# Up-projections of a two-layer diffusion backbone: the order in which ScalarE, VectorE and GpSimd prepare operands and weights

## The chip, the cores and the metric

The kernel runs on one core of one Trainium2 chip. The metric is the device time of one execution in microseconds (us), the median of several runs; less is better. The engines are TensorE (PE, matmuls), VectorE (DVE), ScalarE (ACT), GpSimd (POOL) and SyncE (SP), which issues the DMAs. Each engine works through its own queue in order.

## What is computed

A backbone of two layers over 1024 latent tokens and, in layer 0, 256 context tokens, all fp32, of width 1024. Each layer has an attention mixer and then a channel mixer with a convolution over neighbouring tokens, each behind a modulated RMSNorm:

```python
def conv_ffn(h, w_up, conv_w, conv_b, w_down):
    a = h @ w_up                       # 1024 -> 2 x 2816
    g, u = a[..., :D_FF], a[..., D_FF:]
    T = g.shape[1]
    half = CONV_W // 2                 # CONV_W = 3
    gp = jnp.pad(g, ((0, 0), (half, half), (0, 0)))
    acc = conv_b + gp[:, 0:T] * conv_w[0]
    for j in range(1, CONV_W):
        acc = acc + gp[:, j:j + T] * conv_w[j]
    return (jax.nn.silu(acc) * u) @ w_down

# in each layer i, behind the attention mixer:
ml = (silu(c) @ w_mod[i] + b_mod[i]).reshape(B, N_MOD, 1, D)
xl = xl + ml[:, 5] * conv_ffn(modulate(xl, ml[:, 3], ml[:, 4]), ffn_w_up[i], ...)
if not last:                           # layer 0 alone: the context tokens too
    xc = xc + mc[5] * conv_ffn(modulate(xc, mc[3], mc[4]), ffn_w_up[i], ...)
```

The change touches the product `h @ w_up` of both layers.

## The kernel before

**Products.** A value of fp32 is held as two parts of reduced precision, high and low, and a product is three matmuls: high by high, high by low, low by high (`mm3`, L72). The high part is a cast, the low part the value less its high part. The up-projection works on 22 blocks f of 128 features of g and the same of u. For the latent tokens one block is a 2 x 2 product (g and u by two halves of 512 tokens), computed by Strassen's scheme in Winograd's form with seven products of twelve matmuls each instead of eight. The operand's four sums t1 to t4 are made once, in the head, by four objects `Parts` (one for each row of blocks j): `first` makes four sums in place on DVE (L1598 to L1601), `high` a high half on ACT (L1606, L1608), `low` a low half on DVE (L1616, L1618). The weights' sums s1 to s4 are made for each block: GpSimd adds (L1694), ACT takes the high part (L1698), DVE the low one (L1702). The table of products is

```python
PROD = {1: ("a11", "b11", "x"), 2: ("a12", "b21", "x"), 6: ("s2", "t2", "y"), 7: ("s3", "t3", "y"), 4: ("a22", "t4", "y"), 5: ("s1", "t1", "z"), 3: ("s4", "b22", "z")}
```

with the weight, the operand and the group x, y or z of PSUM banks that takes the sum. There are eight banks, used in a ring. In a trace `y<-h,s3h` is product 7, `z<-h,s4h` product 3, `x<-h,a1h` product 1 or 2, `p<-` a plain product. In layer 0 the context tokens have two plain products in each block.

**A turn.** `Up.turn(f)` writes the order of one block: products 6, 5, 7, then product 1 of the next block, 3, 2 of the next block, 4. Between them stand the steps that bring the sums out of PSUM: `c21` (L1997), `u2` (L1979), `u3` (L1988), `c22` (L1991), `c12` (L1994) on DVE, `s1` (L1975) and `c11` on ACT; the convolution `conv` (ACT, L2004) and `conv2` (DVE, L2008 and L2009), `silu` (ACT, L2012) and `mix` (silu by u; GpSimd for the latent tokens, DVE for the context's, L2015). A finished block is stored to `d_act`. The next block's weights are loaded as two halves `raw` (1024 columns each, two buffers); `ahigh` makes a1h on GpSimd and a2h on ACT, `alow` makes a1l and a2l on DVE (L1683). Product 7 needs u2 to have read its bank, product 3 needs c22 to have read its bank, product 1 of the next block needs a1h and a1l.

**mod().** Layer 0's turns also compute columns of the modulation for later: a DMA brings a block of w_mod into the one buffer `wm`, DVE reduces it (L321, one or two reductions for a block), and GpSimd finishes with steps on one column (L326). `mod()` stands three times in a turn of layer 0.

**The head.** `Up.head` does blocks 0 and 1 with plain products, while the norm in front is still being finished: `n1.quick` makes the last of the operand, and then the `Parts` are made and the turns begin with f = 2. Its `f0` and `f1` are blocks 0 and 1; `gate` (L1969) and `upper` (L1972) copy plain products out of PSUM on ACT. In front of the head stand the last steps of the attention's out-projection, the norm's totals and roots (`n1.split`, `n1.total`, `n1.root`), the splitting of the first two weights `w0[0]` and `w0[1]` (L111 is a low part) and `up.second`, which loads and splits the weights of block 1.

**Order.** Head and turns lie in a region whose order on PE, DVE, ACT and GpSimd is that of the code. The DMA queue of SP lies outside of it and is ordered by a scheduler from the program.

## Time and profile before

| | |
|---|---|
| time, median of 3 runs | 2918.14 us (2915.58 to 2920.52) |
| profiled execution | 2918.13 us, span 2916.3 us, mean granted clock 0.986 |
| TensorE busy | 2793.6 us, 96% of the span, 14654 matmuls |
| DVE, ACT, GpSimd busy | 2201.5 (75%), 1242.3 (43%), 1075.8 (37%) |
| half of a weight block, raw, from issue to landing | 3.3 us in the median of 86 |
| modulation block, wm, from issue to landing | 3.6 us in the median of 72 |

The span runs from the first to the last instruction of the profiled execution; all places named in the text are us from its start. The up-projection of layer 0 lies at about 703 to 1320, that of layer 1 at about 2192 to 2655. An engine's busy time says only that it worked; what a change can win is seen from where TensorE waited, and for whom. The granted clock is a share of TensorE's full speed: where it is under 1, matmuls take longer.

### The profile page before, as it was taken

The numbers are of one execution on the slowest core, as the hardware profiler recorded it, in microseconds if no ns is written. First come the engines' busy times: TensorE is split into PE (matmuls) and PEld (weight loads), VectorE is DVE, ScalarE is ACT, GpSimd is POOL, SyncE is SP. The second block draws the span as 40 slices with busy tenths as digits, with TensorE's granted clock in tenths as the row PEclk, the third lists the DMA queues.
The fourth block names the chain that finished last, engine by engine and source line by source line (L and its number), as shares of the span: only waits on it lengthen the run. The fifth ranks groups of instructions, "written<-read, shape, count | busy, mean of one in ns | idle before, by whom it ended". The sixth has DMA issues, their size and how long they took to land.

```text
span 2916.3 us, 40138 instructions
## 1 busy us (share of the span) xinstructions
PE 2793.6 (96%) x14654; PEld 2319.8 (80%) x14654; DVE 2201.5 (75%) x3646; ACT 1242.3 (43%) x2520; POOL 1075.8 (37%) x1066
## 2 busy tenths in 40 slices
PE   7988999999899999999999998999999999999997
PEld 3857888887778878888888776999977788887886
DVE  5688888879677777668767888888757666558766
ACT  5525888724323323331101444888734333333104
POOL 2142444762234444431101534444331444542112
PEclk9999999999999999999999999999999999999998
DMA  6144001372133433454211110000041222226311
GB/s 227 70 141 137 15 24 58 111 252 100 47 128 106 135 121 105 136 176 165 87 57 48 44 37 30 1 1 1 23 140 51 84 76 84 80 88 234 98 58 58
DMA packets 97230, 264.89 MB, mean 91 GB/s; under 512 B 11909, under 2 KB 21061, under 8 KB 96905
## 3 DMA queue, kind: packets, MB, share of 16 engines
q1 hardware_dynamic: 97032, 262.33, 26.8%
q8 instruction: 115, 1.88, 0.3%
q14 instruction: 83, 0.67, 0.1%
HBM read 212.53 MB, written 49.75 MB: 90 GB/s over the span
## 4 chain that ended last, share of the span: by engine, by line
PE 56%; DVE 11%; ACT 3%; issue 3%; DMA 2%; POOL 1%; DVEq 0%; SPq 0%; ACTq 0%; POOLq 0%
PE d L72 18%; PE y L72 7%; PE x L72 6%; PE z L72 5%; PE p L72 5%; PE pv L1277 3%; PE b L72 3%; DMA wm<-in_wmod 2%; PE T L1264 2%; PE S L1197 1%; PE qk L72 1%; PE S L1199 1%; PE S L1198 1%; DVE x L2008 1%; DVE x L321 1%
## 5 line engine op out<-in xcount | busy, mean ns | idle before, releaser
L2091 DVE SCALAR_TENSOR_TENSOR x<-d,mod,x 128x512 f32<-128x512 f32 (+1 forms) x352 | 254.7, 735 | 94.9 <-PE d L72 92.4
L1246 POOL TENSOR_SCALAR p<-p,sm 128x1280 f32<-128x1280 f32 x128 | 171.3, 1339 | 288.1 <-DVE sm L1245 201.0
L1267 DVE TENSOR_TENSOR tl<-T,th 128x512 fp32r<-128x512 f32 x328 | 225.5, 688 | 46.9 <-ACT th L1266 41.9
L1277 PE MATMUL pv<-th,v 128*128 128x256 f32 x976 | 254.1, 309 | 1.4 <-ACT vo L1406 1.0
L1220 DVE TENSOR_REDUCE mx<-S 128x1 f32<-128x512 f32 (+1 forms) x400 | 234.0, 585 | 10.9 <-PE S L1199 3.7
L72 PE MATMUL d<-act,wh 128*128 128x512 f32 (+1 forms) x832 | 232.0, 365 | 0.0
L1266 ACT CAST th<-T 128x512 fp32r<-128x512 f32 x328 | 192.2, 586 | 84.4 <-PE T L1264 77.0
L2074 ACT CAST act<-act 128x512 fp32r<-128x512 f32 (+1 forms) x110 | 61.4, 577 | 382.8 <-PE d L72 250.4
L72 PE MATMUL b<-h,wh 128*128 128x512 f32 (+1 forms) x752 | 206.6, 362 | 6.0 <-DVE h L489 4.1
L1694 POOL TENSOR_TENSOR x<-raw 128x512 f32<-128x512 f32 x80 | 119.5, 1493 | 237.2 <-DMA raw<-in_wup 136.1
L2015 POOL TENSOR_TENSOR su<-x,su 128x512 f32<-128x512 f32 x78 | 125.9, 1616 | 218.3 <-ACT x L2012 123.7
L72 PE MATMUL x<-h,a1h 128*128 128x512 f32 x624 | 201.2, 404 | 5.0 <-POOL a1h L1678 5.0
L1975 ACT COPY su<-x 128x512 f32<-128x512 f32 x40 | 23.5, 586 | 411.0 <-PE x L72 378.9
L1264 PE MATMUL T<-ident,p 128*128 128x128 f32 x1280 | 193.0, 272 | 1.6 <-POOL p L1246 1.6
L1264 PEld LDWEIGHTS T<-ident,p 128*128 128x128 f32 x1280 | 156.5, 140 | 34.9 <-POOL p L1246 3.3
L1277 PE MATMUL pv<-tl,v 128*128 128x256 f32 x656 | 177.4, 282 | 0.0
L1277 PEld LDWEIGHTS pv<-th,v 128*128 128x128 f32 x976 | 173.4, 189 | 2.4 <-ACT vo L1406 1.5
L72 PEld LDWEIGHTS d<-act,wh 128*128 128x128 f32 x832 | 149.7, 189 | 27.1
L72 PEld LDWEIGHTS b<-h,wh 128*128 128x128 f32 x752 | 132.9, 189 | 35.9 <-DVE h L489 5.5
L72 PE MATMUL d<-act,wl 128*128 128x512 f32 (+1 forms) x416 | 151.8, 365 | 0.0
L72 PEld LDWEIGHTS x<-h,a1h 128*128 128x128 f32 x624 | 120.5, 194 | 34.3 <-POOL a1h L1678 7.1
L72 PE MATMUL x<-h,a1l 128*128 128x512 f32 x312 | 128.1, 411 | 19.4 <-DVE a1l L1683 19.4
(515 smaller groups left out, 8198.0 us busy)
## 6 DMA issues: line engine op xcount, KB each, us to landing
raw<-in_wup SPq DMA_DIRECT2D x86, 512.0 KB, 3.3
wm<-in_wmod SPq DMA_DIRECT2D x72, 512.0 KB, 3.6
act<-d_act SPq DMA_DIRECT2D x88, 256.0 KB, 3.5
raw<-in_wdn SPq DMA_DIRECT2D x44, 512.0 KB, 4.1
raw<-in_wout SPq DMA_DIRECT2D x32, 512.0 KB, 3.4
d_act<-su SPq DMA_DIRECT2D x22, 640.0 KB, 3.5
d_act<-su SPq DMA_DIRECT2D x22, 512.0 KB, 2.8
raw<-in_win SPq DMA_DIRECT2D x20, 512.0 KB, 3.6
```

The costliest lines, as they stand in the source:

```text
L72: PE.matmul(out, w, x, start=first and i == 0, stop=last and i == n - 1, skip_group_check=more)
L321: V.tensor_tensor_reduce(out=out, in0=wm, in1=silc[w], op0=ALU.mult, op1=ALU.add, scale=1.0, scalar=bmod[:, l, i : i + 1], accum_out=mod[l ...
L1220: V.reduce_max(mx[:, j : j + 1], s, axis=AX.X)
L1246: P.tensor_scalar(out=self.p, in0=self.p, scalar1=sm[:, 3:4], scalar2=1.0, op0=ALU.mult, op1=ALU.mult)
L1264: PE.transpose(tb[:, (2 * j + i) * 128 : (2 * j + i) * 128 + 128], rows[i].p[:, c : c + 128], ident)
L1266: S.copy(hi, tb)
L1267: V.tensor_sub(lo, tb, f32(hi))
L1277: PE.matmul(out[0], st, mv, start=(u + j == 0 and x == 0), stop=(u + j == n - 1 and x == len(ops) - 1))
L1694: eng.tensor_tensor(out=t, in0=self.src(f, x), in1=self.src(f, y), op=op)
L2015: eng.tensor_mul(self.s_of(c), self.t[c], self.s_of(c) if u is None else u)
L2074: S.copy(hi, f32(lo))
L2091: V.scalar_tensor_tensor(out=x, in0=b, scalar=mod[self.l, c // 2][:, 40 + d : 41 + d], in1=x, op0=ALU.mult, op1=ALU.add)
```

## The change

No instruction is added or removed; four places of code are written in another order.

- In front of the head, `w0[1]`'s split moves ahead of `n1.split`, and `n1.total` and `n1.root` move ahead of `mod2(3)` and `up.second`.
- In the head, after the quick norm, only the first copies are made (three in layer 0, one in layer 1); then come all four `Parts`, with the copies of f1's gate between the second and the third; then the other copies, a1's two parts, and f1's upper copies.
- In a turn, the load of the next block's first half and its a1h on GpSimd move ahead of the two mixes, and a1l moves to right behind `u2`.
- On SP, in five turns of layer 0, the load of raw's second half now stands ahead of the store to `d_act`.

```diff
--- before.py
+++ after.py
@@ -1782,31 +1782,30 @@
                 b.append(lambda b=self.plain(w1[0], 2): f1.gate(2, b))
             n1.rest()
             n1.quick(())
-            for f in b:
-                f()
-            f0.gate(1, self.plain(w[0], 1, n1.QUICK))
-            f0.upper(1, self.plain(w[1], 1))
-            self.a_tiles()
-            self.ahigh(2, 0, S)
+            b.append(lambda b=self.plain(w[0], 1, n1.QUICK): f0.gate(1, b))
+            b.append(lambda b=self.plain(w[1], 1): f0.upper(1, b))
+            for _ in range(3 if ctx else 1):
+                b.pop(0)()
             parts = [Parts(self, j) for j in range(4)]
             big = lambda: tuple(hp.tile([128, 512], F32R, name="h", tag="h", bufs=HB) for _ in "hl")
             small = lambda: tuple(np_.tile([128, 512], F32R, name="t", tag=t, bufs=tmp.bufs[t]) for t in self.pairs.pop(0))
-            for p in parts[:2]:
+            for j, p in enumerate(parts):
                 p.first()
-                p.high(2, big())
-                p.high(1, big())
-                p.low(2)
-                p.low(1)
+                if j == 2:
+                    for _ in range(2 if ctx else 1):
+                        b.pop(0)()
+                for t in (2, 1):
+                    p.high(t, big() if j < 2 else small())
+                for t in (2, 1):
+                    p.low(t)
+            for f in b:
+                f()
+            self.a_tiles()
+            self.ahigh(2, 0, S)
+            self.alow(2, 0)
             f1.upper(0, self.plain(w1[1], 0))
             if ctx:
                 f1.upper(2, self.plain(w1[1], 2))
-            self.alow(2, 0)
-            for p in parts[2:]:
-                p.first()
-                p.high(2, small())
-                p.high(1, small())
-                p.low(2)
-                p.low(1)
             if ctx:
                 t = self.sp.tile([128, 1024], F32, name="wm", tag="wm", bufs=1)
                 f0.temps = [t[:, :512], t[:, 512:]]
@@ -1863,13 +1862,15 @@
                 down.load(0)
                 for e in (0, 1):
                     down.act_load(e)
+            if n:
+                self.load(n, 0)
+                self.ahigh(n, 0, P)
             if f > 2:
                 old.mix(1)
                 old.mix(0)
                 old.store()
             self.alow(f, 1)
             if n:
-                self.load(n, 0)
                 self.load(n, 1)
             else:
                 down.load(1)
@@ -1877,6 +1878,8 @@
             if not n:
                 down.act_split(0)
             me.u2()
+            if n:
+                self.alow(n, 0)
             if f == 2:
                 old.rest()
                 me.c11(True)
@@ -1884,9 +1887,6 @@
                 if f == 3 and not ctx:
                     self.fs[0].rest()
                 self.mod()
-            if n:
-                self.ahigh(n, 0, P)
-                self.alow(n, 0)
             self.product(f, 7)
             if not n:
                 down.act_split(1)
@@ -2246,13 +2246,13 @@
     o.update(15, 1)
     up.spill(7, 1)
     last()
+    w0[1] = w0[1]()
     n1.split()
+    up.plain(w0[0], 0, range(6, 8), b00)
+    n1.total()
+    n1.root()
     mod2(3)
     up.second(1)
-    up.plain(w0[0], 0, range(6, 8), b00)
-    n1.total()
-    w0[1] = w0[1]()
-    n1.root()
     up.second(0)
     up.head(w0, b00, n1)
     for f in range(2, NF):
@@ -2880,12 +2880,12 @@
     o.update(15, 1)
     up.spill(7, 1)
     last()
+    w0[1] = w0[1]()
     n1.split()
-    up.second(1)
     up.plain(w0[0], 0, range(6, 8), b00)
     n1.total()
-    w0[1] = w0[1]()
     n1.root()
+    up.second(1)
     up.second(0)
     up.head(w0, b00, n1)
     for f in range(2, NF):
```

ACT in the head of layer 0, behind the quick norm. `p` is a plain product in PSUM, g and su are the rows of a block, L1606 and L1608 write high halves of the `Parts`:

```order
-L1969 COPY g<-p 128x512
-L1969 COPY g<-p 128x256
-L1969 COPY g<-p 128x512
-L1972 COPY su<-p 128x512
-L1676 CAST a1h<-raw 128x1024
 L1606 ACTIVATE h<-x_6972,mod_65 128x512
 L1608 CAST h<-x_6972 128x512
 L1606 ACTIVATE h<-x_6973,mod_65 128x512
 L1608 CAST h<-x_6973 128x512
-L1972 COPY su<-p 128x512
-L1972 COPY su<-p 128x256
+L1969 COPY g<-p 128x512
```

Four copies and a1h, which stood ahead of the first high halves, now stand behind them.

ACT in the head of layer 1, at the end of the `Parts`:

```order
 L1606 ACTIVATE t<-x_12641,mod_66 128x512
 L1608 CAST t<-x_12641 128x512
+L1969 COPY g_21844<-p 128x512
+L1972 COPY su_21841<-p 128x512
+L1676 CAST a1h<-raw 128x1024
+L1972 COPY su<-p 128x512
 L1969 COPY g<-p 128x512
 L1698 CAST s2h<-x_22104 128x512
```

Here three copies and a1h now follow the last high half of the fourth `Parts`.

GpSimd in a turn of layer 0, between the sum s4 of one block (first row) and the first sum of the next (last row). L2015 is `mix`:

```order
 L1694 TENSOR_TENSOR x_8412<-raw,x_8413 128x512
-L2015 TENSOR_TENSOR su<-x_8547,su 128x512
-L2015 TENSOR_TENSOR su<-x_8546,su 128x512
-L1678 TENSOR_SCALAR a1h<-raw 128x1024
+L1678 TENSOR_SCALAR a1h<-raw 128x1024
+L2015 TENSOR_TENSOR su<-x_8547,su 128x512
+L2015 TENSOR_TENSOR su<-x_8546,su 128x512
 L1694 TENSOR_TENSOR x_8413<-raw 128x512
```

a1h has passed both mixes.

DVE in the same turn, around u2 (L1979). The rows of L321 are a reduction of `mod()` and its step behind it:

```order
 L1683 TENSOR_TENSOR a2l<-raw,a2h 128x1024
 L1979 TENSOR_TENSOR x_8546<-y,su 128x512
+L1683 TENSOR_TENSOR a1l<-raw,a1h 128x1024
 L321 ISA wm,mod_66<-wm,silc_7007,bmod 128x1024
 L321 ISA mod_66 128x1
-L1683 TENSOR_TENSOR a1l<-raw,a1h 128x1024
 L1988 TENSOR_TENSOR su<-y,su 128x512
```

a1l has passed the reduction and follows u2.

## Rows read from the trace of the kernel before

**Rows 1.** The table by stretches: the stretch and its length in us, busy time of each engine (with its number of instructions), the granted TensorE clock as a share of full speed, the busy share of the DMA engines and GB/s.

```profile
770.00:801.08 31.08, 21.80 (x84) 17.34 (x83) 25.14 (x33) 13.98 (x25) 11.12 (x10) 0.78 0.29 100
...
808.00:1030.00 222.00, 214.38 (x1095) 177.65 (x1094) 167.31 (x225) 68.53 (x115) 93.67 (x89) 1.00 0.37 122
...
1030.00:1200.00 170.00, 160.00 (x801) 131.19 (x799) 121.72 (x164) 49.88 (x84) 83.42 (x91) 0.98 0.36 121
...
2300.00:2640.00 340.00, 339.49 (x1467) 275.41 (x1465) 206.54 (x265) 116.37 (x198) 165.37 (x157) 1.00 0.26 89
```

**Rows 2.** The timeline of TensorE (PE) in the head of layer 0. Columns of this and of all timelines below: start, length in us, engine, line, operation, output<-inputs, shape, number of like instructions in a row, and in brackets the idle time just before it with what ended it. Each row is the first matmul of a product or the one that waited.

```profile
709.61 0.50 PE L72 MATMUL p<-h,wl 128*128 128x512 f32 x1 [3.34 <-DVE wl L111]
...
772.51 0.63 PE L72 MATMUL z<-h,s1h 128*128 128x512 f32 x2
...
779.79 1.19 PE L72 MATMUL y<-h,s3h 128*128 128x512 f32 x2 [4.33 <-DVE x L1979]
...
790.81 0.80 PE L72 MATMUL x<-h,a1l 128*128 128x512 f32 x1 [4.95 <-DVE a1l L1683]
...
798.29 0.63 PE L72 MATMUL z<-h,s4h 128*128 128x512 f32 x2
...
801.08 0.62 PE L72 MATMUL x<-h,a1h 128*128 128x512 f32 x2
```

**Rows 3.** The timelines of VectorE (DVE) and ScalarE (ACT) in the same head, in order of time.

```profile
724.50 0.69 DVE L1598 TENSOR_TENSOR x<-x,x 128x512 f32<-128x512 f32 x1
...
742.36 1.05 ACT L1676 CAST a1h<-raw 128x1024 fp32r<-128x1024 f32 x1
...
744.06 0.75 DVE L1616 SCALAR_TENSOR_TENSOR h<-x,mod,h 128x512 fp32r<-128x512 f32 x1 [16.70 <-ACT h L1606]
...
745.33 0.69 DVE L1598 TENSOR_TENSOR x<-x,x 128x512 f32<-128x512 f32 x1
...
749.54 1.22 DVE L1683 TENSOR_TENSOR a1l<-raw,a1h 128x1024 fp32r<-128x1024 f32 x1
...
769.41 0.58 ACT L1972 COPY su<-p 128x512 f32<-128x512 f32 x1
...
778.96 0.68 DVE L1979 TENSOR_TENSOR x<-y,su 128x512 f32<-128x512 f32 x1
...
791.39 0.69 DVE L1991 TENSOR_TENSOR su<-z,su 128x512 f32<-128x512 f32 x1
```

**Rows 4.** The timeline of TensorE in layer 0: the first matmuls of product 7 (y<-h,s3h), one for a turn, at the ends of the stretches that the prediction speaks of.

```profile
815.10 0.63 PE L72 MATMUL y<-h,s3h 128*128 128x512 f32 x2
...
1028.48 0.70 PE L72 MATMUL y<-h,s3h 128*128 128x512 f32 x2
...
1059.08 0.70 PE L72 MATMUL y<-h,s3h 128*128 128x512 f32 x2 [0.53 <-DVE x L1979]
...
1196.93 0.63 PE L72 MATMUL y<-h,s3h 128*128 128x512 f32 x2
...
1222.21 0.63 PE L72 MATMUL y<-h,s3h 128*128 128x512 f32 x2
```

**Rows 5.** The timelines of DVE, TensorE and GpSimd (POOL) around the parts of a1, in an early and in a late turn of layer 0.

```profile
868.77 1.64 DVE L321 CUSTOM_DVE_ANT_0 x<-wm,silc,bmod 128x1024 bf16<-128x1024 f32 x1 [0.98 <-DMA wm<-in_wmod]
...
872.94 0.50 PE L72 MATMUL x<-h,a1l 128*128 128x512 f32 x1 [1.51 <-DVE a1l L1683]
...
1031.01 1.51 POOL L326 TENSOR_SCALAR mod<-mod 128x1 f32<-128x1 f32 x2 [2.13 <-DVE mod L321]
...
1032.49 1.04 POOL L1678 TENSOR_SCALAR a1h<-raw 128x1024 fp32r<-128x1024 f32 x1
...
1033.58 0.74 PE L72 MATMUL x<-h,a1h 128*128 128x512 f32 x2 [2.07 <-POOL a1h L1678]
```

**Rows 6.** The timeline of DVE in a turn of layer 0: u2, the reduction over wm, and u2 of the turn behind it.

```profile
894.50 0.69 DVE L1979 TENSOR_TENSOR x<-y,su 128x512 f32<-128x512 f32 x1
...
902.52 1.29 DVE L321 CUSTOM_DVE_ANT_0 x<-wm,silc,bmod 128x1024 bf16<-128x1024 f32 x1 [2.23 <-DMA wm<-in_wmod]
...
920.79 0.69 DVE L1979 TENSOR_TENSOR x<-y,su 128x512 f32<-128x512 f32 x1
```

**Rows 7.** The timelines of POOL and DVE in a turn of layer 0, and one row of DVE in the head of layer 1.

```profile
860.05 1.28 POOL L2015 TENSOR_TENSOR su<-x,su 128x512 f32<-128x512 f32 x1 [3.63 <-ACT x L2012]
...
860.41 1.21 DVE L2008 SCALAR_TENSOR_TENSOR x<-g,convw,x 128x256 f32<-128x256 f32 x1 [1.19 <-ACT x L2004]
...
2242.36 1.67 DVE L1599 TENSOR_TENSOR x<-x 128x512 f32<-128x512 f32 x1
```

**Rows 8.** The timelines of DVE and TensorE in the head of layer 1 and the first turn behind it.

```profile
2222.14 0.69 DVE L1598 TENSOR_TENSOR x<-x,x 128x512 f32<-128x512 f32 x1
...
2239.33 0.64 PE L72 MATMUL x<-h,a1h 128*128 128x512 f32 x2
...
2259.12 0.70 PE L72 MATMUL y<-h,s3h 128*128 128x512 f32 x2 [3.00 <-DVE x L1979]
...
2268.27 0.69 DVE L1991 TENSOR_TENSOR su<-z,su 128x512 f32<-128x512 f32 x1
...
2272.12 1.06 PE L72 MATMUL z<-h,s4h 128*128 128x512 f32 x2
...
2292.23 0.50 PE L72 MATMUL x<-h,a1l 128*128 128x512 f32 x1 [2.09 <-DVE a1l L1683]
```


## The prediction

> **What bounds the kernel now.** TensorE is busy 96% of the span, so a change of order can only win where TensorE stands still or runs below its full clock. I read the table by stretches first. In the up-projection of layer 1, from 2300 to 2640, TensorE is busy 339.49 of 340 us [rows 1]: nothing is to be had there. In layer 0 it is idle 7.6 us of 808 to 1030 and 10.0 us of 1030 to 1200, and the head (770 to 801.08) leaves 9.3 us idle with a granted clock of 0.78 [rows 1]. So four places matter: the layer-0 head, its early turns, its late turns, and the layer-1 head.
>
> Next, TensorE's own timeline in the layer-0 head [rows 2]. It waits 3.34 us at 709.61 for the low half of w0[1] (DVE, L111), then 4.33 at 779.79 for u2 (L1979) and 4.95 at 790.81 for a1l (L1683). A wait costs more than itself: after it the matmuls run at a lower clock for a while. An undisturbed product of twelve matmuls takes 2.79 (798.29 to 801.08). From 772.51 to 801.08 stand four products and a context product (24 matmuls of half the columns), which is 5 x 2.79 = 13.95 undisturbed, and they take 28.57: 14.6 are lost. With the stall at 709.61 (3.34, some 1.7 for slow matmuls behind it, less 0.4 of DVE work that stays ahead) that makes 14.6 + 4.6 = 19.2, the most that this head can give.
>
> Who is late is seen on DVE and ACT [rows 3]. DVE finishes the first subtractions of the first `Parts` after 724.50 and then stands 16.70 us, until 744.06, for a high half from ACT (L1606). ACT in turn has f0.gate(1), f0.upper(1) and a1h (742.36) ahead of it in its queue, copies that wait for TensorE's plain products. One `Parts` costs DVE 4.2 (745.33 to 749.54), so all that follows, down to f1.upper(1) (769.41) and u2 (778.96), inherits the 16.70.
>
> In the turns I read the starts of y<-h,s3h [rows 4]. The last turn shown, 1196.93 to 1222.21, has no stall and takes 25.28. The eight turns from 815.10 to 1028.48 take 213.38 against 8 x 25.28 = 202.24; the six to 1196.93 take 168.45 against 151.68. So 11.1 and 16.8 us are lost.
>
> **The change part by part.** Nothing is added or removed; TensorE's order is the same. All of it is worked from the profiled execution, 2918.13 us, which equals the median of the runs.
>
> *Ahead of the head, layer 0.* w0[1]'s split now precedes n1's on DVE. That removes the stall at 709.61: TensorE is 4.8 earlier (3.34 + 1.7 - 0.4, rounded up for latency). The norm's chain gets DVE 0.8 later, so the `Parts` start at 724.50 + 0.8 = 725.3.
>
> *Layer-0 head.* ACT now takes the `Parts`' high halves before the copies that wait, so DVE does four `Parts` in a row: 725.3 + 4 x 4.2 + 2.0 (GpSimd's sums collide with the third, twice some 1.0, see the lock below) = 744.1. Then a1h to 745.3 and a1l to 746.6; TensorE, 4.8 earlier, wants them only after 750.9, so the 16.70 is used up with 4.3 to spare. f1.upper(1) then hangs on TensorE alone: 769.41 less 4.8 and less the 5 that ACT no longer lags, 759.6. u2 came 9.6 after that copy; without the a1l work in between 8.7, hence 768.3 to 769.0. TensorE wants it at 772.51 - 4.8 + 2.79 = 770.5: the 4.33 goes, and a1l, now right behind u2, comes at 770.6, so the 4.95 goes too. Late next is c22 (L1991), 12.4 behind u2 (778.96 to 791.39): 781.3 to 782.2. z<-h,s4h has to wait for it, and TensorE is there at 770.5 + 3 x 2.79 = 778.9. A new wait of 2.5 to 3.3 plus about 1.5 of slow matmuls. z<-h,s4h ends at 785.7 to 786.6 instead of 801.08: **gain 15**. Bounds: 19.2 if c22 also moves up; 11 if u2 does not come clear of TensorE.
>
> *Early turns.* Turns alternate by how many reductions over wm (L321) fall where. In one kind, a double reduction waits for its DMA (868.77), a1l comes after it, and TensorE stops 1.51 at 872.94 [rows 5]. With a1l right behind u2 that wait goes. In the other kind TensorE is not the limit: u2 at 894.50, the single wm buffer comes free after it, its DMA lands 8.0 later (902.52, 2.23 waited), the double reduction follows, and the next u2 is at 920.79: a loop of DVE and DMA of 26.29 [rows 6], which the change does not shorten. The new price is a lock between DVE and GpSimd [rows 7]: a mix of GpSimd at 860.05 (1.28 us, to 861.33) holds up a DVE step of conv2 over only 256 columns, 1.21 us long and ending at 861.62, just behind it; in layer 1 a DVE subtraction next to GpSimd work took 1.67 where others like it take 0.69 (745.33 [rows 3]). With a1h (1.04) [rows 5] ahead of mix(1) (1.28), two GpSimd instructions stand where one stood. Bounds per turn: 0.4 earlier, if the mix slips behind conv2 and only a1h collides; 0.9 later, if both do. I take 0.6, since each collision in the rows lasted as long as GpSimd's instruction. So the first kind takes 25.28 + 0.6 + 0.2 of latency = 26.1, the second 26.3 + 0.4 = 26.7; four of each are 211.2 against 213.4: **gain 2**, bounds -3 (0.9 in each turn, nothing from a1l) and +9 (no lock cost, loop looser).
>
> The Trainium skill ("SBUF — State Buffer", section Who interferes with whom) speaks against this move: a DVE instruction with two SBUF inputs and a GpSimd instruction that reads SBUF exclude each other, and whoever starts first holds the shared ports for its whole length. The trace agrees in the 1.21 and the 1.67; by the rule alone the sum would take 0.9 in every turn, and the early turns would gain nothing.
>
> *Late turns.* From 1028.48 on, GpSimd's a1h stands behind small steps on mod (L326) that wait for DVE's reduction (2.13 at 1031.01); a1h starts at 1032.49 and TensorE stops 2.07 at 1033.58 [rows 5], in a turn of 30.60 [rows 4]. With a1h ahead of the mixes it is ready before the reduction. Three turns of the first kind at 26.1 and three of the second at 25.4 to 26 make 155 against 168.45: **gain 13.5**, bounds 9 and 16.8 (all that is lost there).
>
> *Five stores on SP* now stand behind a load of raw instead of ahead: no wait of TensorE in these turns ends on a store or on that load, which the mixes and the sums of a later turn cover; cost nothing. If that cover were gone, each would cost one load's landing, 3.3 us in the page's list of issues.
>
> *Layer-1 turns* gain nothing [rows 1].
>
> *Layer-1 head.* Here the norm's chain is pushed by 1.2 (two sums' low halves now stand ahead of it), and TensorE waits for its result already, so TensorE is 1.2 late; the `Parts` start at 2222.14 + 1.2 [rows 8] and end at 2223.3 + 4 x 4.2 + 2.0 = 2242.2. Only then come two copies and a1h (2243.3) and a1l (2244.6). TensorE wants x<-h,a1h at 2239.33 + 1.2 = 2240.5: a new wait of 3.6 and 1.6 of slow matmuls. y<-h,s3h starts at 2263.2, 4.1 after 2259.12, its 3.00 wait on u2 gone. c22 came 9.15 after that start, so z<-h,s4h starts at 2263.2 + 9.15 + 0.9 = 2273.2 against 2272.12, 0.9 more for clock; the 2.09 wait of the turn behind (2292.23, 2.4 with latency) goes. **Net about 0**, bounds -4 and +4.
>
> Sum: 15 + 2 + 13.5 + 0 = 30.5, so 2918.1 - 30.5 = 2888.
>
> **The rivals.** *More comes back (gain 38 to 47, 2871 to 2880).* The lock falls the other way: a1h runs early, the mixes slip behind conv2, so u2 comes sooner in every turn, and c22 in the head too. For it: GpSimd has idle time in front of its first mix (3.63 at 860.05 [rows 7]). Against: the loop over wm is not shortened. *Given back (gain 10 to 22, 2896 to 2908).* The a1 waits turn into u2 waits: DVE's order u2, a1l, reduction makes the reduction, and so the next wm load, 1.2 later, and the loop of 26.29 becomes 27.5 in half the turns. For it: the loop already bounds those turns; against: in half of them the reduction waits for its DMA anyway. This takes 8 to 12 from the sum. *Nothing moves (within 0.2%, 5.8 us, about what a measurement can tell from no change).* Heads lose in layer 1 and in the late turns what they gain in layer 0. Against: the 16.70 and the 2.07 are plain. *Slower (gain -6 to -15, 2924 to 2933).* In the new head f0.gate(1), f0.upper(1) and f1.gate(0) leave PSUM only after the `Parts`; if their eight banks run out, TensorE stands at a product with nowhere to write. f0.gate(1) was copied by 742.36 and will be by about 744, and TensorE needs its bank near 765: 21 us to spare (15 in layer 1). It decides only where the `Parts` run more than that late, and costs what they are late beyond it, 35 us or more together.
>
> **How the numbers follow.** The forecast (gain 25 to 37) has 0.45, more back 0.20, given back 0.25, nothing 0.06, slower 0.04. Faster by over 0.2% is 0.45 + 0.20 + 0.25 = 0.90. The time is 2888; the range 2874 to 2905 leaves out the slow tail (0.1) and the far end of the gains (0.07).
>
> **What would show it.** Right: no wait on L111 near 709; no DVE idle of more than 2 us between 725 and 744; z<-h,s4h of the layer-0 head near 783 with a wait on c22 (L1991); starts of y<-h,s3h 26 to 27 apart with no wait on a1l or a1h, the late turns no slower than the early ones; conv2 rows stretched over 1 us. In layer 1 a wait on a1l near 2241, and 2300 to 2640 unchanged. Wrong: u2 waits of over 1 us in each turn (given back), or a wait of TensorE for a PSUM bank in either head (slower).

## The result, and the profile after

The changed kernel takes 2892.29 us (median of four runs, 2890.34 to 2894.36) against 2918.5 for the kernel before in the same comparison (four runs, 2915.58 to 2920.52): a ratio of 0.9911, with a 95% interval of 0.9894 to 0.9928. It is 26 us faster, where 30.5 were forecast, and lies inside the range. Its profiled execution has a span of 2891.4, which is 24.9 less than before, and a mean granted clock of 0.989.

The table by stretches of the changed kernel, with the columns of [rows 1]: the end of layer 0's head, the eight early and the six late turns, the end of layer 1's head, and layer 1's turns.

```profile
768.02:786.68 18.66, 15.77 (x74) 13.10 (x72) 17.83 (x22) 6.28 (x12) 5.95 (x9) 0.91 0.20 73
800.67:1014.15 213.48, 203.72 (x1058) 171.46 (x1056) 166.10 (x217) 65.91 (x112) 86.22 (x88) 1.00 0.38 123
1014.15:1170.44 156.29, 153.78 (x793) 130.09 (x793) 122.00 (x161) 49.74 (x84) 81.20 (x90) 0.99 0.39 129
2210.00:2256.00 46.00, 37.05 (x134) 28.57 (x133) 30.09 (x38) 19.88 (x33) 12.35 (x13) 0.85 0.13 46
2300.00:2612.00 312.00, 312.00 (x1349) 253.41 (x1348) 191.19 (x241) 105.49 (x180) 158.97 (x145) 1.00 0.25 87
```

TensorE's idle time in the late turns fell from 10.0 of 170 us to 2.5 of 156, and its clock stands at 0.99. The early turns have 9.8 us idle of 213.5, some 2 more than before (7.6 of 222 in [rows 1]). The head of layer 1 has a clock of 0.85 and 9 us idle of 46. Layer 1's turns are full, as in [rows 1].

**Layer 0's head.** Timelines of all engines, the rows that answer to [rows 2, 3]:

```profile
700.03 0.50 PE L72 MATMUL p<-h,wl 128*128 128x512 f32 x1 [0.57 <-DVE wl L111]
...
725.52 0.69 DVE L1598 TENSOR_TENSOR x<-x,x 128x512 f32<-128x512 f32 x1
...
743.67 0.69 DVE L1618 TENSOR_TENSOR t<-x,t 128x512 fp32r<-128x512 f32 x1
...
759.80 0.59 ACT L1972 COPY su<-p 128x512 f32<-128x512 f32 x1 [5.29 <-PE p L72]
...
769.30 0.68 DVE L1979 TENSOR_TENSOR x<-y,su 128x512 f32<-128x512 f32 x1
...
781.49 0.69 DVE L1991 TENSOR_TENSOR su<-z,su 128x512 f32<-128x512 f32 x1
...
782.32 1.19 PE L72 MATMUL z<-h,s4h 128*128 128x512 f32 x2 [2.89 <-DVE su L1991]
...
786.68 0.63 PE L72 MATMUL x<-h,a1h 128*128 128x512 f32 x2
```

The wait on wl is 0.57, at an earlier weight. The four `Parts` run without a break from 725.52 to 744.3, u2 (769.30) is in time, and what is late next is c22 at 781.49: TensorE waits 2.89 for it in front of z<-h,s4h. The product behind it starts at 786.68, 14.4 before the 801.08 of [rows 2].

**An early turn.** GpSimd, DVE and TensorE in the turn that ends at 880.08, and a reduction of the turn behind it, to be held against [rows 6, 7]:

```profile
865.52 0.68 DVE L1994 TENSOR_TENSOR g<-z,x 128x512 f32<-128x512 f32 x1
...
870.20 1.05 POOL L1678 TENSOR_SCALAR a1h<-raw 128x1024 fp32r<-128x1024 f32 x1 [3.44 <-DMA raw<-in_wup]
...
870.73 0.78 DVE L2008 SCALAR_TENSOR_TENSOR x<-g,convw,x 128x256 f32<-128x256 f32 x1 [1.19 <-ACT x L2004]
...
871.21 1.46 POOL L2015 TENSOR_TENSOR su<-x,su 128x512 f32<-128x512 f32 x1
...
871.55 1.40 DVE L2009 SCALAR_TENSOR_TENSOR x<-g,convw,x 128x256 f32<-128x256 f32 x1
...
879.25 0.69 DVE L1979 TENSOR_TENSOR x<-y,su 128x512 f32<-128x512 f32 x1
...
879.85 1.70 DVE L1683 TENSOR_TENSOR a1l<-raw,a1h 128x1024 fp32r<-128x1024 f32 x1
...
880.08 0.70 PE L72 MATMUL y<-h,s3h 128*128 128x512 f32 x2 [1.16 <-DVE x L1979]
...
887.44 2.31 DVE L321 CUSTOM_DVE_ANT_0 x<-wm,silc,bmod 128x1024 bf16<-128x1024 f32 x1 [2.88 <-DMA wm<-in_wmod]
```

a1h waits for its load (3.44) and starts just ahead of mix(1). Both meet the convolution of the context: its second step (L2009) takes 1.40. From c12 (865.52) to u2 (879.25) DVE needs 13.73, and TensorE waits 1.16 for u2. In the turn behind it a reduction still waits 2.88 for its block wm.

**The late turns**, with [rows 4, 5]:

```profile
1014.15 0.70 PE L72 MATMUL y<-h,s3h 128*128 128x512 f32 x2 [1.43 <-DVE x L1979]
...
1037.11 1.52 POOL L326 TENSOR_SCALAR mod<-mod 128x1 f32<-128x1 f32 x2 [8.38 <-DVE mod L321]
...
1038.59 1.05 POOL L1678 TENSOR_SCALAR a1h<-raw 128x1024 fp32r<-128x1024 f32 x1
...
1041.45 1.06 PE L72 MATMUL y<-h,s3h 128*128 128x512 f32 x2 [1.84 <-DVE x L1979]
...
1170.44 0.63 PE L72 MATMUL y<-h,s3h 128*128 128x512 f32 x2
```

No wait of TensorE on a1h or a1l is left. In the first of these turns GpSimd's small steps on mod (L326) still stand ahead of a1h, but they wait for a reduction at the end of the turn before, not for one behind u2, and a1h is there in time; what TensorE waits for is u2 (1.84).

**Layer 1's head**, with [rows 8]:

```profile
2215.35 0.30 PEld L72 LDWEIGHTS x<-h,a1h 128*128 128x128 f32 x2 [2.94 <-ACT a1h L1676]
...
2216.75 0.29 PEld L72 LDWEIGHTS x<-h,a1l 128*128 128x128 f32 x1 [1.10 <-DVE a1l L1683]
...
2227.53 0.59 ACT L1972 COPY su<-p 128x512 f32<-128x512 f32 x1 [10.22 <-PE p L72]
...
2228.77 0.75 DVE L1616 SCALAR_TENSOR_TENSOR h<-x,gap,h 128x512 fp32r<-128x512 f32 x1 [10.66 <-ACT h L1606]
...
2236.49 0.68 DVE L1979 TENSOR_TENSOR x<-y,su 128x512 f32<-128x512 f32 x1
...
2246.73 0.69 DVE L1991 TENSOR_TENSOR su<-z,su 128x512 f32<-128x512 f32 x1
...
2247.57 1.19 PE L72 MATMUL z<-h,s4h 128*128 128x512 f32 x2 [4.43 <-DVE su L1991]
```

The weight loads of x<-h,a1h wait 2.94 and 1.10 for a1h and a1l, which now come behind the `Parts`. Then ACT stands 10.22 at f1.upper(1), a copy of a plain product that TensorE has not made yet, with the high halves 3 and 4 of the `Parts` behind it, and DVE stands 10.66 for the first of those. u2 and c22 follow from there, and TensorE waits 4.43 for c22 in front of z<-h,s4h.

### The profile page after: what moved, and what is told of

It is laid out like the page before. It is cut to its first block, busy times and chain, and to the rows that moved or that the text cites. A ratio compares the mean times of both kernels' runs of the same rounds, so it can differ in the third digit from the quotient of the medians.

```text
span 2891.4 us, 40143 instructions
## 1 busy us (share of the span) xinstructions
PE 2781.4 (96%) x14654; PEld 2316.9 (80%) x14654; DVE 2214.3 (77%) x3646; ACT 1240.3 (43%) x2520; POOL 1072.3 (37%) x1066
## 4 chain that ended last, share of the span: by engine, by line
PE 58%; DVE 10%; ACT 3%; issue 2%; DMA 1%; POOL 1%; DVEq 0%; SPq 0%; ACTq 0%; POOLq 0%
PE d L72 18%; PE y L72 9%; PE x L72 6%; PE z L72 6%; PE p L72 5%; PE pv L1277 3%; PE b L72 3%; PE T L1264 2%; PE S L1197 1%; PE S L1199 1%; PE S L1198 1%; PE qk L72 1%; DVE x L2009 1%; DVE x L2008 1%; DMA wm<-in_wmod 1%
## 5 line engine op out<-in xcount | busy, mean ns | idle before, releaser
L2015 POOL TENSOR_TENSOR su<-x,su 128x512 f32<-128x512 f32 x78 | 140.5, 1813 | 79.5 <-DVE su L1997 67.0
L1237 ACT ACTIVATE p<-S,mx,rq 128x512 f32<-128x512 f32 (+1 forms) x192 | 136.2, 712 | 12.6 <-DVE mx L1228 11.1
```

Of the source, the lines that this page charges most:

```text
L1237: S.activation(o, s, AF.Exp, scale=self.scale, bias=self.mx[:, 3:4], accum_out=self.sm[:, j : j + 1])
L2015: eng.tensor_mul(self.s_of(c), self.t[c], self.s_of(c) if u is None else u)
```

## The experiments

Each kernel ran beside the kernel before on the same chip. That kernel took 2913.86 in the first group of four, 2912.33 in the second and 2914.95 (median of seven) in the last, so times are compared inside a group. Stages are compared by starts of products in the trace: s1 is the first p<-h,s1h of a head, z its first z<-h,s4h, the early and late turns run between the product-7 starts of [rows 4], and the layer-1 column is from s1 to the third y<-h,s3h.

| kernel | time | beside it, before | s1, layer 0 | s1 to z | 8 early turns | 6 late | layer 1 |
|---|---|---|---|---|---|---|---|
| before (profile) | 2918.13 | | 722.08 | 76.21 | 213.38 | 168.45 | 98.05 |
| changed (profile) | 2893.38 | | 717.59 | 64.73 | 213.48 | 156.29 | 101.65 |
| ahead_l0 | 2913.13 | 2913.86 | 717.79 | 76.75 | 212.85 | 167.09 | 100.36 |
| head_l0 | 2904.07 | 2913.86 | 717.33 | 71.16 | 212.96 | 166.52 | 98.46 |
| turns_only | 2895.06 | 2913.86 | 722.76 | 70.27 | 211.27 | 154.22 | 95.43 |
| l1_only | 2920.70 | 2913.86 | 722.83 | 76.29 | 212.46 | 167.26 | 105.05 |
| a1h_alone | 2902.59 | 2912.33 | 717.58 | 70.12 | 215.42 | 157.83 | 101.66 |
| a1l_alone | 2894.38 | 2912.33 | 717.28 | 64.74 | 208.03 | 159.40 | 104.18 |
| mix_swap | 2914.37 | 2912.33 | 717.52 | 64.75 | 223.51 | 159.49 | 105.58 |
| copy_late | 2883.01 | 2912.33 | 716.31 | 63.63 | 213.39 | 153.22 | 95.74 |
| l1_fix | 2877.01 | 2914.95 | 718.22 | 63.65 | 210.69 | 153.94 | 90.64 |
| mod_early | 2882.29 | 2914.95 | 718.19 | 64.73 | 206.63 | 152.95 | 101.21 |
| best | 2871.35 | 2914.95 | 719.54 | 63.66 | 205.25 | 152.87 | 90.69 |

One thing shows how far single figures carry: the turns of the changed kernel, copy_late, l1_fix and turns_only are the same code, and their eight early turns took 213.48, 213.39, 210.69 and 211.27. Differences of 2 us in that column mean little. The same four agree in the late turns within 3.1.

### The parts of the change, one at a time

**ahead_l0** is the kernel before with this edit alone:

```diff
+    w0[1] = w0[1]()
     n1.split()
+    up.plain(w0[0], 0, range(6, 8), b00)
+    n1.total()
+    n1.root()
     mod2(3)
     up.second(1)
-    up.plain(w0[0], 0, range(6, 8), b00)
-    n1.total()
-    w0[1] = w0[1]()
-    n1.root()
     up.second(0)
```

> The kernel before with one part of the change: in front of layer 0's head, w0[1]'s split ahead of the norm's, the norm's total and root ahead of the rest. Theory (the head passes the stall on undiminished): TensorE's wait of 3.34 on wl at 709.61 is gone, all of the head is 4.8 earlier, since f0.upper(1) and a1h wait for TensorE; z<-h,s4h of the head starts at 793.5 instead of 798.29, the waits of 4.33 and 4.95 stay, and the time is 2913. Rival (the head absorbs it): the waits on u2 and a1l grow by the same, 798.29 stays, time 2918.

The head starts 4.3 earlier and keeps 3.8 of it to z (794.54): s1 to z is 76.75 against 76.21. The stages follow the theory, the time doesn't show it: beside it there are 0.7 us, and the 2913 came out because the kernel before took 2913.86 here. One run of each can't tell a few us, so the theory rests on the stages.

**head_l0** adds the new head, in layer 0 alone (the diff is the first of the change, under `if ctx`).

> The kernel before with the change in layer 0 up to the end of the head (the order in front of it and the head), the turns and layer 1 as before. Theory: z<-h,s4h of the head starts near 782.3 as with the whole change, with its wait on c22; the early turns take what they took before (213.4 for eight), the late ones too (168), so the gain is 14.4 and the time 2904. Rival: the late turns also lose their 12, because they were late from the head, and the time is 2892.

The time came out as forecast, but not for the reason: the gain on the same chip is 9.8, not 14.4. s1 to z fell by 5.6 from 76.75, not by 12. The rest of the head's gain isn't in the head's code. The late turns keep their 166.5, so the rival falls.

**turns_only** is the kernel before with the new `turn` alone.

> The kernel before with the new order of the turns alone. Theory: eight early turns 213.5 (no change, the wait on a1l turned into one on u2), six late turns 156.3 instead of 168.45, layer 1's turns unchanged; but turn 3 of layer 1 loses its wait of 2.09, so the time is 12 to 14 less, 2905. Rival: without the new head the late turns stay at 168 and the time at 2918.

It gains 18.8, more than both theories said. The late turns do what the theory said (154.22), and so does layer 1: its column falls by 2.6, most of it the wait of 2.09 in turn 3. The surprise is in layer 0's head: s1 to z falls by 5.9, since the head's last a1l belongs to `turn(2)`, where it moved ahead of all of block 1's `old.rest()`.

**l1_only** has the new order in layer 1's head alone (and in front of it).

> The kernel before with the new order in front of layer 1's head and in that head alone. Theory: it loses. The copies behind the Parts make a1h and a1l late (TensorE waits 2.9 and 1.1 at x<-h,a1h), and the head and first turns take 3.6 to 5 us more, time 2922. Rival: the head alone costs nothing and the loss seen with the whole change comes from the turns' new order: 2918.

It loses 6.8 on the same chip, and 5 to 7 in its own column (105.05 against 98.1 to 100.4 in the kernels with the old order there). The theory has the direction right, but the loss is dearer than its 3.6 to 5 and than in the whole change, where the turns' part gives 3 back. The order in front of the head and the head itself aren't told apart by this run.

### What the turns gain and lose

**a1h_alone**: the changed kernel, a1l back behind the reduction.

```diff
             me.u2()
-            if n:
-                self.alow(n, 0)
             if f == 2:
                 old.rest()
                 me.c11(True)
             else:
                 self.mod()
+            if n:
+                self.alow(n, 0)
```

> The changed kernel with a1l on DVE put back behind the reduction, so that in the turns only the load and a1h on GpSimd are moved. Theory (a1h ahead of the small steps on mod is what the late turns gain from): six late turns stay near 156 to 158; in the early ones the wait on a1l comes back where a double reduction stands (1.5 at product 1), beside the wait on u2 of 1.2, so eight take 214 to 218. Rival (a1l's place is what counts): late turns back at 165 or more.

Late turns 157.83: a1h's place ahead of the mixes, with its load, alone makes 9.5 to 10.6 of the 12 to 13 (against the mean of the old order and against the profile before). Early turns 215.42, with the waits on a1l back in the double turns. And in the head TensorE waits for the a1l that is again behind `old.rest()`, here on the timeline of TensorE:

```profile
780.75 0.79 PE L72 MATMUL x<-h,a1l 128*128 128x512 f32 x1 [6.53 <-DVE a1l L1683]
```

s1 to z is 5.4 longer than with the change. So of the 16.0 by which z moved up, about 4.5 come from the order in front, 5.6 from the head's own and 5.9 from a1l's place in `turn(2)`.

**a1l_alone**: the changed kernel, a1h back behind the mixes (the load stays ahead of them).

```diff
             if n:
                 self.load(n, 0)
-                self.ahigh(n, 0, P)
             if f > 2:
                 old.mix(1)
                 old.mix(0)
@@
             me.u2()
             if n:
+                self.ahigh(n, 0, P)
                 self.alow(n, 0)
```

> The changed kernel with a1h on GpSimd put back behind the mixes, so that in the turns the load and a1l are moved, a1l waiting for a1h on DVE. Theory: conv2 meets one instruction of GpSimd again, so c12 to u2 is 0.5 shorter (13.25 with the double reduction instead of 13.73), but DVE stands 1 to 2 us behind u2 until a1h is made, and the reduction and the next load of wm are later by it: early turns 213 to 216, late 158 to 162. Rival: the load ahead of the mixes alone makes a1h early enough and all is as with the change (213.5 and 156.3).

GpSimd and DVE in one of its early turns:

```profile
863.49 0.68 DVE L1994 TENSOR_TENSOR g<-z,x 128x512 f32<-128x512 f32 x1
...
868.35 1.29 POOL L2015 TENSOR_TENSOR su<-x,su 128x512 f32<-128x512 f32 x1 [3.62 <-ACT x L2012]
...
868.71 1.22 DVE L2008 SCALAR_TENSOR_TENSOR x<-g,convw,x 128x256 f32<-128x256 f32 x1 [1.19 <-ACT x L2004]
...
869.96 0.48 DVE L2009 SCALAR_TENSOR_TENSOR x<-g,convw,x 128x256 f32<-128x256 f32 x1
...
876.75 0.68 DVE L1979 TENSOR_TENSOR x<-y,su 128x512 f32<-128x512 f32 x1
...
879.01 1.22 DVE L1683 TENSOR_TENSOR a1l<-raw,a1h 128x1024 fp32r<-128x1024 f32 x1 [1.58 <-POOL a1h L1678]
```

Now only the mix meets the convolution: L2008 takes 1.22 and L2009 0.48, and c12 to u2 is 13.26 (863.49 to 876.75) where the change has 13.73. DVE does stand 1.58 for a1h behind u2, but in a place where it has much of that time: the reduction waited there for its DMA before the change (0.98 at 868.77 [rows 5]). So the early turns take 208.03, less than either theory said and 2.7 to 5.5 less than with the change; eight times the 0.5 of the chain is 4 of that. By this one run, what takes the early turns' gain is that both instructions of GpSimd meet the convolution. The late turns (159.40, inside the theory's 158 to 162) and layer 1 (104.18) lose by it, so that the time beside it gains only 18.0.

**mix_swap**: the changed kernel with the two mixes exchanged.

```diff
-                old.mix(1)
                 old.mix(0)
+                old.mix(1)
                 old.store()
```

> The changed kernel with mix(0), which waits for c21, ahead of mix(1), so that only a1h meets conv2 of the context on DVE. Theory (the lock costs the early turns their gain): L2009 over 256 columns falls from 1.40 to 0.48, c12 to u2 from 13.73 to 12.8 and from 12.42 to 11.5, the waits on u2 shrink, and eight early turns take 206 to 209 instead of 213.5, unless the second mix, now next to a1l and the reduction, gives half of it back; time 2885 to 2890. Rival (the loop over wm sets the pace): the early turns stay within 1 us of 213.5, time 2892.

Both theories miss, by another mechanism. DVE, GpSimd, ACT and SP (SPq, the issue of a DMA) in two of its early turns:

```profile
929.75 0.48 DVE L2009 SCALAR_TENSOR_TENSOR x<-g,convw,x 128x256 f32<-128x256 f32 x1
...
940.01 0.33 SPq L2033 DMA_DIRECT2D d_act<-su  x1
940.44 0.37 SPq L1644 DMA_DIRECT2D raw<-in_wup  x1
...
945.46 0.59 ACT L1975 COPY su<-x 128x512 f32<-128x512 f32 x1 [13.21 <-DMA d_act<-su]
...
946.58 1.29 POOL L1694 TENSOR_TENSOR x<-raw 128x512 f32<-128x512 f32 x1 [6.59 <-DMA raw<-in_wup]
...
950.22 0.62 ACT L1698 CAST s2h<-x 128x512 fp32r<-128x512 f32 x1 [3.72 <-POOL x L1694]
```

The same steps in the changed kernel:

```profile
934.08 0.33 SPq L2033 DMA_DIRECT2D d_act<-su  x1
934.51 0.37 SPq L1644 DMA_DIRECT2D raw<-in_wup  x1
...
939.33 1.29 POOL L1694 TENSOR_TENSOR x<-raw 128x512 f32<-128x512 f32 x1 [5.27 <-DMA raw<-in_wup]
```

The lock's price goes as forecast (L2009 at 0.48; c12 to u2 is 12.7 to 12.9 with the double reduction). But mix(0) waits for c21 and mix(1) now stands behind it, so the store of the block is issued 2.64 behind the start of product 7 (937.37), where the changed kernel issues it 0.41 behind (933.67). On SP's queue the load of raw's second half stands behind that store. GpSimd waits 6.59 for this load, and ACT 3.72 for GpSimd's sum, before the next high parts; in the changed kernel the same high part comes without a wait. c12 comes 14.0 to 16.7 behind product 7 in all early turns but the first, against 12.1 to 13.8. ACT's copy s1 does wait for the store (13.21), but in the changed kernel it waits 9.7 to 11.0 for TensorE at the same place, and here the high parts behind it wait longer still for the load. The turns take up to 29.4. That the lock costs the change its early gain is borne out here by the two lengths only; the early turns answer to the load behind the store, as far as these rows show. Half of what this run loses lies in later stages (layer 1's column is 105.58), and why isn't shown.

### Mending what the profile shows

**copy_late**: the changed kernel, f1.upper(1) behind the high halves.

```diff
-            f1.upper(1, self.plain(w1[1], 1))
+            b = self.plain(w1[1], 1)
             ...
             for j, p in enumerate(parts):
                 p.high(3, big() if j < 2 else xs(j - 2))
                 p.low(3)
                 if j < 2:
                     p.high(4, big())
                     p.low(4)
+            f1.upper(1, b)
```

> The changed kernel with f1.upper(1), the copy for which ACT waits 10 us in each head, behind the high halves 3 and 4 of the Parts. Theory: this copy is what makes DVE late in both heads (DVE idle 10.66 before 2228.77 in layer 1), as the copies of f0 were before the change: z<-h,s4h of layer 0 loses its wait of 3.1 (4.6 with slow matmuls), and in layer 1 the waits on u2 and c22 shrink, 5 to 8 together; time 2880 to 2884. Rival: c22 hangs on the convolutions and mixes of block 0 or 1 on DVE, not on that copy: within 2 us of the changed kernel.

The time is 29.3 under that of the kernel before on its chip, where the change was 26.2 under its own; that 2883 lies in the theory's range owes something to a kernel before that took 2912.33 here. Layer 1's column falls by 5.9, as the theory said. In layer 0 s1 to z falls by only 1.1, not by 3: counted from s1, u2 comes only 1.1 earlier (ACT waits 2.31 for TensorE at its next copy, at 761.43, ahead of s3h), and c22 stands 12.15 behind u2, with DVE's work for block 1 between them. For that part the rival is right.

**l1_fix** adds to copy_late, in layer 1, a1's parts beside the third `Parts` (shown here), and the old order in front of its head.

```diff
                 if j == 2:
                     for _ in range(2 if ctx else 1):
                         b.pop(0)()
+                    if not ctx:
+                        self.a_tiles()
+                        self.ahigh(2, 0, S)
                 ...
+                if j == 2 and not ctx:
+                    self.alow(2, 0)
             for f in b:
                 f()
-            self.a_tiles()
-            self.ahigh(2, 0, S)
-            self.alow(2, 0)
+            if ctx:
+                self.a_tiles()
+                self.ahigh(2, 0, S)
+                self.alow(2, 0)
```

> The changed kernel with f1.upper(1) behind the Parts' high halves 3 and 4 in both heads, and in layer 1 a1h on ACT and a1l on DVE beside the third of the Parts instead of behind the fourth, and the order in front of the layer-1 head as before the change. Theory (in layer 1 the change lost by a1's parts behind all four Parts and by the norm's chain 1.2 later): TensorE's waits on a1h (2.9) and a1l (1.1) in that head go, and from the first s1 product to the third product 7 it takes 91 to 94 us, against 101.7 with the change, 98.1 before it and 95.7 with the copy alone moved. Rival (the loss is the Parts' own length on DVE): 95 to 97, because u2 and c22 then come later by what a1l takes.

ACT, DVE and TensorE in its layer-1 head:

```profile
2197.23 1.05 ACT L1676 CAST a1h<-raw 128x1024 fp32r<-128x1024 f32 x1
...
2201.84 1.22 DVE L1683 TENSOR_TENSOR a1l<-raw,a1h 128x1024 fp32r<-128x1024 f32 x1
...
2220.56 0.69 DVE L1986 TENSOR_TENSOR x<-y,su 128x512 f32<-128x512 f32 x1 [0.34 <-PE y L72]
...
2231.63 1.19 PE L72 MATMUL z<-h,s4h 128*128 128x512 f32 x2 [2.78 <-DVE su L1998]
```

a1l is done at 2203, TensorE comes to it at 2206.5 without a wait, u2 waits for TensorE instead of the other way round, and only the wait on c22 (2.78) is left. The column is 90.64, a little better than the theory's 91 to 94 and 11 less than with the change. The copy alone gave 5.9 of these 11 in copy_late; the other two edits aren't told apart.

**mod_early**: the changed kernel, with the turn's third reduction ahead of the context's convolution.

```diff
             for c in self.chunks:
                 if c == 2:
+                    self.mod()
                     me.conv(2)
                     me.conv2(2)
                 me.silu(c)
             ...
             if ctx:
                 me.mix(2, V, self.bank[f, "c", 1])
-                self.mod()
```

> The changed kernel with the third reduction of a layer-0 turn moved from the turn's end to ahead of the convolution of the context, where DVE waits 1.2 us for ACT. Theory (after the change the early turns are bounded by the chain on DVE from c12 to u2, 13.73 and 12.42 us long, with the lock in it): the chain shrinks by about 1.2 in both kinds of turn, the waits on u2 go, eight early turns take 203 to 207 instead of 213.5. Rival (the loop over the one wm buffer sets the pace): its loads start earlier too, but the turns stay at 26.5 or more, 212 to 214.

DVE in one of its early turns:

```profile
863.06 0.68 DVE L1994 TENSOR_TENSOR g<-z,x 128x512 f32<-128x512 f32 x1
...
868.33 1.93 DVE L321 CUSTOM_DVE_ANT_0 wm<-wm,silc,bmod 128x1024 f32<-128x1024 f32 x1
...
875.98 0.68 DVE L1979 TENSOR_TENSOR x<-y,su 128x512 f32<-128x512 f32 x1
```

c12 to u2 is 12.92 instead of 13.73 (11.6 instead of 12.4 in the other kind): 0.8 of the 1.2, since the reduction itself takes 1.93 in its new place, where it took 1.28. Eight early turns take 206.63, in the theory's range, and the rival as it was put falls. So the chain on DVE from c12 to u2 was part of what bounded the early turns after the change. The loop over wm isn't ruled out by it: the chain is a part of that loop, and in the changed kernel c12 still follows, in every second turn, a reduction that waited for wm (2.88 at 887.44).

**best** is l1_fix and mod_early together.

> The last two together: the copy and the layer-1 head mended and the third reduction early. Theory: the stages add up: layer 0's head 2.4 better than with the change, the early turns 7, the late ones 3 to 5, layer 1's head 7 to 9, so some 20 less than the changed kernel and 45 less than before: 2870 to 2875, a ratio of 0.984 to 0.986 to the kernel before. Rival: early turns unmoved, 2880.

2871.35 (four runs, 2869.80 to 2874.47) against 2914.95 (seven, 2911.72 to 2917.51): 0.9853, interval 0.9836 to 0.9869, which lies below the change's 0.9894 to 0.9928. Against the changed kernel's profile the early turns give 8.2, the late ones 3.4 and layer 1 11.0, as forecast or better. Layer 0's head gives 1.1 from s1 to z, not 2.4, and s1 itself stands 2.0 later in this run.

## Why the prediction came out

| step | forecast | measured in the profiles | 
|---|---|---|
| in front of layer 0's head (a part of the next row) | 4.8 | 4.5 (s1 at 722.08, then 717.59) |
| all of layer 0's head | 15 | 14.4 (801.08, then 786.68) |
| early turns | 2 | -0.1; 0.7 by the means of four kernels with each order |
| late turns | 13.5 | 12.2; 12.9 by the same means |
| layer 1's head | 0 | -3.6 (98.05, then 101.65) |
| sum | 30.5 | 22.9 |

The remaining 2.0 of the span's 24.9 lie where nothing was moved: 1.4 of them between layer 0's turns and layer 1's head, where the kernels above scatter from 910.1 to 912.7.

**Layer 0's head was right step by step.** `Parts` were forecast for 725.3 to 744.1 and ran 725.52 to 744.3, with the collisions in the place of [rows 7]; c22 was forecast to end at 781.3 to 782.2 and ends at 782.2; the new wait was put at 2.5 to 3.3 and is 2.89. What the text didn't see is which edit the end of it hangs on: it has a1l "right behind u2" but books it under the head, and the 5.4 (a1h_alone) to 5.9 us (turns_only) of it come from `turn(2)`.

**Late turns: right**, as to the mechanism and within 1.3 us. a1h alone makes most of it.

**Early turns: the lock's price was right, what it does to TensorE only in part.** 0.6 was taken for each turn (the sum uses 0.4 in the second kind, without a reason); c12 to u2 grew by 0.48 (from 13.25, which ends at the 894.50 of [rows 6], to 13.73) and 0.50 (from 11.92, which ends at 920.79 there, to 12.42). But the wait on a1l did not simply go. It became one on u2 (1.16 at 880.08), because the double-reduction turns are bounded on DVE as soon as c12 to u2 is longer than TensorE takes; I had put that into the other kind alone. The forecast of 26.1 for this kind is 26.63 in the turn that ends at 880.08, and the other's 26.7 is 26.89. The rule cited there (the Trainium skill, "SBUF — State Buffer", Who interferes with whom) would have given no gain in these turns, and it is nearer the -0.1 to 0.7 that were measured than the 2 of the sum; but the 0.9 for each turn that the forecast took by it is further from the 0.5 measured than 0.6 is, so that this is in part luck. The bound of -3 doesn't follow from its own terms either: 0.9 in each of eight turns is 7.

**Layer 1's head is the term that failed**, within its bounds of -4 to +4 but at their end. The norm's chain did what was forecast: TensorE waits 1.0 more for it behind s1, where 1.2 was put. Three things were mis-sized. The wait on a1's parts was put at 3.6 and the slow matmuls after it at 1.6, 5.2 together, but the three products around it take 14.65 instead of 8.28, so they cost 6.4 (the weight loads wait 2.94 + 1.10). u2's wait was said to vanish, but f1.upper(1) hangs on TensorE's own delayed product (10.22 on ACT), so 1.6 of it stays (the product ahead of it takes 4.41 for 2.79). And z<-h,s4h, behind its wait of 4.43, takes 5.25 for 2.79, where I had 0.9 more. One sum was off too: 1.2 + 3.6 + 1.6 - 3.0 is 3.4, not the 4.1 by which y<-h,s3h was to start later. Counted from s1 it starts 6.1 later. l1_only shows the head's own price as 5 to 7, and turns_only the turns' gain there as 2.6 (3.5 against the mean of the kernels with the old order).

**The stores** were said to cost nothing, and in the changed kernel they don't show in the turns. But the cover that was named, the mixes and sums of a later turn, is thin: in mix_swap the last mix ends 2.2 us later against product 7, the load behind the store is later by as much, and the turn is longer by up to 2.6. In the changed kernel itself ACT waits 3.50 on a store once in layer 0's head and 5.35 in layer 1's, off the path both times, as far as the rows show.

The rival "given back" (8 to 12 from the turns) did not come in the time, though the sign named for it did: TensorE waits over 1 us for u2 in seven of the eight early turns (1.16 to 1.43). That sign couldn't tell the two apart, since a wait on a1l of about that length (1.51) went in half the turns. "More back" did not come either, since both GpSimd instructions met the convolution.

## What to carry to other kernels

Where an in-order engine makes operands for TensorE, look for copies in its queue that wait for TensorE itself: a copy at the head of a queue holds back all that other engines wait for, here 16.70 us before the change and 10.66 in the place that the change left. The same order isn't good in two places that differ in slack: behind the `Parts`, a1's halves were free in layer 0 (a1l is done 4.4 us before TensorE comes to it) and cost TensorE 6.4 us in layer 1. An operation moved ahead on GpSimd should be held against what DVE does at that time, against the store that ends the row behind it, and against the loads that stand behind that store in SP's queue.

## What the runs showed of the hardware

DVE's work beside GpSimd's was stretched in each early turn looked at, and not by the same operation each time: L2009 over 256 columns took 0.48 alone and 1.40 beside a mix, a1l over 1024 columns 1.22 alone and 1.70 (879.85) beside one. After a wait of 4.43 us a product of twelve matmuls took 5.25 us instead of 2.79, and the one behind it 3.02. The table by stretches of the changed kernel for these two, with the columns of [rows 1]:

```profile
2247.57:2252.82 5.25, 5.25 (x12) 4.11 (x13) 1.90 (x3) 2.76 (x5) 1.60 (x1) 0.50 0.02 6
2252.82:2255.84 3.02, 3.02 (x13) 2.44 (x12) 2.74 (x4) 0.72 (x1) 0.00 (x0) 0.91 0.50 176
```

The first ran wholly at a granted clock of 0.50, the lower level of 1.2 GHz, the second at 0.91, mostly back at 2.4 GHz. The wait of 2.89 in layer 0's head cost 1.57 in the same way (z<-h,s4h from 782.32 to 786.68, at a granted clock of 0.62), but the waits of 1.2 to 1.4 for u2 in seven of the eight early turns left the clock at 1.00. The same code's early turns differed by 2.8 us of 213 between runs, while the four stall-free turns behind the late ones took 101.40 to 101.46 in every kernel but mix_swap.
